# The low parts of some weights made by an accumulating DMA instead of VectorE

## The chip, the cores and the metric

The kernel runs on one core of a Trainium2 chip. The metric is the device time of one execution in microseconds, as the median over runs. Engines are named as in the profile: PE (TensorE), ACT (ScalarE), DVE (VectorE), POOL (GpSimd), SP (SyncE, which here only issues DMAs).

## The reference

A decoder trunk of two layers on 512 tokens of width 1024. In each layer the normalised input is multiplied by one wide projection whose columns feed four mixers of 512 channels, each with a gate:

```
h = rms_norm(x, norm_g[layer])
a_u, a_g, qd, kd, vd, b_g, c_x, c_g, m_q, m_g = split(h @ w_in[layer], 10)
y_a = s5_mixer(a_u, ...)            # complex state-space scan, GELU, GLU
y_b = diff_attention(q, k, v, lam)  # two softmaxes, their difference
y_c = rglru_mixer(c_x, ...)         # convolution, gated linear recurrence
y_m = memory_attention(m_q, ...)    # 256 memory tokens
mixed = concat(y_a * silu(a_g), y_b * silu(b_g), y_c * silu(c_g), y_m * silu(m_g))
x = x + mixed @ w_out[layer]
```

A last normalisation gives the output. Everything is float32.

## The kernel before

The large products are made in three passes on PE to keep float32 accuracy: each operand is split into a high part (rounded to the format fp32r) and a low part (what the rounding left), and a product is high x high + high x low + low x high. The activations are split once per layer (hThi, hTlo). The weights are split as they stream in.

The weights come in 136 pieces of 128 partitions x 1024 floats (512 KB), 68 for each layer, in a hand-written order of groups: in layer 0 q v k kv cx au cg bg mq ag mg gl and the output projection, in layer 1 q k cx v kv au mq bg mg ag cg gl and the output projection. cg, bg, mq, ag and mg are the gates and the memory query; each has 4 pieces, so the five have 20 pieces in a layer. They come after au, the input of the state-space mixer, so they are multiplied while that mixer (function s5, with many small VectorE operations on tiles u, xr, xp, wt, kq) runs, and in layer 0 also the end of the attention and the linear recurrence (function lru). A piece of these five groups gives 24 matmuls of 512 columns at L508 (cm_block).

One piece takes this way. SP loads it into a tile raw (two buffers; w_load, L152). ACT rounds it into whi (three buffers; L166). DVE subtracts whi from raw and gives wlo (three buffers; L172). Then raw is free, and SP loads the piece after the next one. When PE comes to piece i, w_use asks for the splits up to piece i+2, so both copies run two pieces ahead of PE; a whi or wlo buffer is free again once PE has left the piece three before.

Side work is written as generators (class Streams) that are stepped between groups of matmuls; each engine then works its instructions in a fixed order made when the program is built. POOL does little: it clears a few tiles, loads block-diagonal weights (bd, L1080), and at L966 issues for each of the four blocks of s5 8 small copies from kq to MT, which wait for DVE's kq.

Of the kernel before, what the change touches and what calls it, by code (L numbers as in the profile page):

```python
# [13 lines left out]
AF = mybir.ActivationFunctionType  # L14
ALU = mybir.AluOpType
# [14 lines left out]

ORDER = ["q v k kv cx au cg bg mq ag mg gl oAM0 oAM1 oBC0 oBC1".split(),
         "q k cx v kv au mq bg mg ag cg gl oAM0 oAM1 oBC0 oBC1".split()]

C_ID, C_DM, C_IF, C_KEEP, C_CM, C_END = 0, 128, 144, 152, 152, 280

# [55 lines left out]
def tile_kernel(ctx: ExitStack, tc: tile.TileContext, A, out):  # L91
    nc = tc.nc
    V, S, G, PE = nc.vector, nc.scalar, nc.gpsimd, nc.tensor
# [11 lines left out]
    def nm(s):  # L105
        uid[0] += 1
        return f"{s}_{uid[0]}"
# [26 lines left out]


    pieces = []
    wbuf = {}
    loaded = [0]
    split = {"hi": 0, "lo": 0}
# [2 lines left out]
    def w_dma(upto):  # L142

        while loaded[0] < min(upto, len(pieces)):
            w_load(loaded[0])
            loaded[0] += 1

    def w_load(i):
        src = pieces[i]
        raw = wpool.tile([P, 1024], F32, tag="raw", bufs=NRAW, name=nm("raw"))  # L150
        if len(src.shape) == 3:
            nc.sync.dma_start(out=raw.rearrange("p (a b) -> p a b", a=src.shape[1]), in_=src)  # L152
        else:
            dst = raw.rearrange("p (a b c) -> p a b c", a=src.shape[1], b=src.shape[2])
            for j in range(src.shape[2]):
                nc.sync.dma_start(out=dst[:, :, j], in_=src[:, :, j])
        wbuf[i] = raw

    def w_split(i, pool_):

        while split[pool_] < min(i + 1, len(pieces)):
            j = split[pool_]
            split[pool_] += 1
            if pool_ == "hi":
                hi = wpool.tile([P, 1024], F32R, tag="whi", bufs=NHI, name=nm("whi"))
                S.copy(hi, wbuf[j])  # L166
                wbuf[j] = (wbuf[j], hi)
            else:
                w_split(j, "hi")
                raw, hi = wbuf[j]  # L170
                lo = wpool.tile([P, 1024], F32R, tag="wlo", bufs=NLO, name=nm("wlo"))
                V.tensor_tensor(out=lo, in0=raw, in1=hi, op=ALU.subtract)  # L172
                wbuf[j] = (hi, lo)
                w_dma(j + NRAW + 1)

    def w_use(i):
        w_split(i + NHI - 1, "hi")
        w_split(i + NLO - 1, "lo")
        return wbuf.pop(i)
# [23 lines left out]
    COL = {n: i * GW for i, n in enumerate(["au", "ag", "q", "k", "v", "bg", "cx", "cg", "mq", "mg"])}  # L203

    def add(l, n, u, ps_):
        plan.append((l, n, u, list(range(len(pieces), len(pieces) + len(ps_)))))
        pieces.extend(ps_)

# [8 lines left out]
    for l in range(DEPTH):  # L217
        for n in ORDER[l]:
            if n == "kv":
                for u in range(2):  # L220
                    add(l, "mk", u, cm_pieces(A["w_mem_kv"][l], 256 * u))
                add(l, "mv", 0, tm_pieces(A["w_mem_kv"][l], 512))
            elif n == "gl":
                w = A["s5_w_glu"][l].rearrange("(k p) (s c) -> p k s c", p=P, s=2)
                for u in range(2):
                    add(l, "gl", u, [w[:, 2 * i:2 * i + 2, :, 256 * u:256 * u + 256] for i in range(2)])
            elif n[0] == "o":
                ps_ = []
                for g in n[1:3]:
                    r0 = 512 * "ABCM".index(g)  # L230
                    ps_ += tm_pieces(w_out[l, r0:r0 + 512], 512 * int(n[3]))
                add(l, "o", n[1:], ps_)
            elif n in ("q", "k", "v", "au"):
                add(l, n, 0, tm_pieces(w_in[l], COL[n]))
            else:
                for u in range(2):
                    add(l, n, u, cm_pieces(w_in[l], COL[n] + 256 * u))
# [24 lines left out]
    for l in range(DEPTH):  # L262
        nc.sync.dma_start(out=vec[65:81, l].rearrange("q (g c) -> q g c", g=2)[:, :, 0:16],
                          in_=A["s5_d"][l].rearrange("(q g) h -> q g h", g=2))
# [53 lines left out]
    for t in range(NT):  # L318
        h, hn = hn, (norm_h(t + 1) if t + 1 < NT else None)
        transpose_split(h, cur["hi"], cur["lo"], t * 128)  # L320
        if t < 2:
            w_split(t, "lo")
# [49 lines left out]
    for bits in (5, 8, 10, 24):  # L372
        e = math.floor(math.log2(rest))
        q = 2.0 ** (e - bits)
        c = math.floor(rest / q) * q if bits != 24 else float(np.float32(rest))
# [726 lines left out]
    for pi, (l, n, u, ids) in enumerate(plan):  # L1102
# [93 lines left out]
        elif n == "gl":  # L1196
# [4 lines left out]
            for hf, pid in enumerate(ids):  # L1201
                whi, wlo = (w.rearrange("p (k s c) -> p k s c", k=2, s=2) for w in w_use(pid))
                for j in range(2):
                    for s in (1, 0):
                        a = gacc[j][s]
# [9 lines left out]
                    if hf == 1:  # L1215
                        V.scalar_tensor_tensor(out=th, in0=th, scalar=1.0, in1=a, op0=ALU.add, op1=ALU.mult)
                        ag = R["ag"][:, 2 * u + j, :]
# [4 lines left out]
        if n == "o":  # L1222
# [29 lines left out]
            hi = lambda k, t, gs=gs: gs[k // 4][0][:, k % 4, t * 128:(t + 1) * 128]  # L1252
            lo = lambda k, t, gs=gs: gs[k // 4][1][:, k % 4, t * 128:(t + 1) * 128]
# [69 lines left out]
```

## Time and profile before

| | us |
|---|---|
| median of 3 runs | 934.51 (934.37 to 934.92) |
| the profiled execution, its own time | 934.99 |
| its span, first to last instruction | 933.2 |
| PE busy | 908.3 (97%) |
| DVE busy | 645.2 (69%) |
| ACT busy | 521.4 (56%) |
| POOL busy | 42.8 (5%) |

A matmul's record overlaps with the next one's, so PE is called busy when it works without a gap; the idle time of PE in a stretch is the stretch less PE's busy time. The shares are means over stages with very different loads, which is why the rows below go by stretches. PEclk is the share of TensorE's full clock that was granted.

### The profile page before, as it was taken

Reading aid. Unit: us, or ns where it says so; the run is one execution under the profiler, and the core shown is the slowest. Engines: PE = TensorE matmul, PEld = TensorE weight load, DVE = VectorE, ACT = ScalarE, POOL = GpSimd, SP = SyncE. Lnnn points to the kernel's source line nnn. Section 1 sums busy time; section 2 is a strip of 40 time slices with the busy share of each in tenths; the row PEclk is TensorE's granted clock in tenths of the full one; section 3 lists DMA queues with packets and bytes.
Section 4 is the critical chain, followed back from the end, with each engine's and each line's share of the span. In section 5 each row is a group of like instructions: output and inputs, shape, how many; then the busy total and the mean of one; then the engine's idle time right before and its main releaser. Section 6 shows DMA issues by size and latency. Waiting matters only on the chain.

```text
span 933.2 us, 12492 instructions
## 1 busy us (share of the span) xinstructions
PE 908.3 (97%) x4538; PEld 751.0 (80%) x4538; DVE 645.2 (69%) x1297; ACT 521.4 (56%) x1038; POOL 42.8 (5%) x94
## 2 busy tenths in 40 slices
PE   6999999999999989999999999999999999999997
PEld 4788878877888878888888888788778888788885
DVE  6975877458999965893373675853698998667343
ACT  6674776987343355831454579665646333764123
POOL 1001000001011100000100000000101110000000
PEclk9999999999999999999999999999999999999999
DMA  5833432103213225532343321421212222243222
GB/s 198 210 103 99 137 91 68 46 23 94 68 50 116 71 69 186 142 113 91 106 162 105 91 91 46 147 89 59 72 48 70 72 72 68 68 155 117 93 88 91
DMA packets 81072, 90.59 MB, mean 97 GB/s; under 512 B 23793, under 2 KB 58226, under 8 KB 81010
## 3 DMA queue, kind: packets, MB, share of 16 engines
q1 hardware_dynamic: 77986, 85.98, 29.8%
q10 hardware_dynamic: 720, 2.62, 0.8%
q0 software_dynamic: 2304, 1.18, 0.5%
q8 instruction: 36, 0.59, 0.3%
q14 instruction: 26, 0.21, 0.1%
HBM read 84.92 MB, written 4.19 MB: 95 GB/s over the span
## 4 chain that ended last, share of the span: by engine, by line
PE 78%; DVE 14%; ACT 4%; DMA 2%; issue 2%; SPq 1%; DVEq 0%; ACTq 0%
PE acc L528 37%; PE acc L508 19%; PE acc L1209 5%; DVE u L340 3%; PE sc L639 2%; DVE wlo L172 2%; PE ms L672 2%; PE tp L1032 1%; PE sc L638 1%; DVE xr L1015 1%; PE sc L640 1%; PE tp L826 1%; PE tp L305 1%; PE tp L662 1%; PE sc L801 1%
## 5 line engine op out<-in xcount | busy, mean ns | idle before, releaser
L166 ACT CAST whi<-raw 128x1024 fp32r<-128x1024 f32 x136 | 143.2, 1053 | 224.4 <-PE acc L528 123.8
L172 DVE TENSOR_TENSOR wlo<-raw,whi 128x1024 fp32r<-128x1024 f32 x136 | 166.1, 1222 | 120.8 <-ACT whi L166 120.3
L508 PE MATMUL acc<-hThi,whi 128*128 128x512 f32 x384 | 155.3, 404 | 0.3 <-DVE bg L709 0.3
L508 PE MATMUL acc<-hThi,wlo 128*128 128x512 f32 x384 | 153.1, 399 | 0.0
L508 PE MATMUL acc<-hTlo,whi 128*128 128x512 f32 x384 | 152.7, 398 | 0.0
L528 PE MATMUL acc<-whi,hThi 128*128 128x512 f32 x256 | 105.1, 410 | 0.8 <-ACT whi L166 0.8
L528 PE MATMUL acc<-wlo,hThi 128*128 128x512 f32 x256 | 101.7, 397 | 0.0
L528 PE MATMUL acc<-whi,hTlo 128*128 128x512 f32 x256 | 101.1, 396 | 0.0
L528 PE MATMUL acc<-whi,mxl 128*128 128x512 f32 x256 | 100.2, 391 | 0.0
L528 PE MATMUL acc<-whi,mxh 128*128 128x512 f32 x256 | 100.2, 391 | 0.0
L528 PE MATMUL acc<-wlo,mxh 128*128 128x512 f32 x256 | 100.2, 391 | 0.0
L508 PEld LDWEIGHTS acc<-hThi,wlo 128*128 128x128 f32 x384 | 72.6, 189 | 14.2
L508 PEld LDWEIGHTS acc<-hThi,whi 128*128 128x128 f32 x384 | 72.7, 189 | 13.5 <-DVE bg L709 0.7
L508 PEld LDWEIGHTS acc<-hTlo,whi 128*128 128x128 f32 x384 | 72.8, 190 | 12.9
L528 PEld LDWEIGHTS acc<-whi,hThi 128*128 128x128 f32 x256 | 56.4, 220 | 8.9 <-ACT whi L166 1.2
L528 PEld LDWEIGHTS acc<-whi,hTlo 128*128 128x128 f32 x256 | 56.3, 220 | 7.7 <-DVE hTlo L308 0.2
L528 PEld LDWEIGHTS acc<-wlo,hThi 128*128 128x128 f32 x256 | 56.6, 221 | 7.1
L528 PEld LDWEIGHTS acc<-whi,mxl 128*128 128x128 f32 x256 | 48.1, 188 | 9.8
L528 PEld LDWEIGHTS acc<-whi,mxh 128*128 128x128 f32 x256 | 48.1, 188 | 9.7
L528 PEld LDWEIGHTS acc<-wlo,mxh 128*128 128x128 f32 x256 | 48.1, 188 | 9.6
L642 DVE TENSOR_REDUCE mx<-sc 128x2 f32<-128x256 f32 (+3 forms) x32 | 26.3, 823 | 36.3 <-PE sc L640 36.2
L966 POOL DMA_DIRECT2D MT<-kq x64 | 32.1, 508 | 376.3 <-DVE kq L340 233.5
(305 smaller groups left out, 1671.5 us busy)
## 6 DMA issues: line engine op xcount, KB each, us to landing
raw<-in_w_in_dram SPq DMA_DIRECT2D x80, 512.0 KB, 3.6
raw<-in_w_out_dram SPq DMA_DIRECT2D x32, 512.0 KB, 3.3
raw<-in_w_mem_kv_dram SPq DMA_DIRECT2D x16, 512.0 KB, 3.3
x<-in_x_dram SPq DMA_DIRECT2D x8, 512.0 KB, 5.2
raw<-in_s_w_glu_dram SPq DMA_DIRECT2D x16, 256.0 KB, 3.1
mt<-in_mem_dram SPq DMA_DIRECT2D x4, 512.0 KB
xd<-x SPq DMA_DIRECT2D x4, 512.0 KB, 4.3
x<-xd SPq DMA_DIRECT2D x4, 512.0 KB, 7.0
```

The costliest lines, as they stand in the source:

```text
L166: S.copy(hi, wbuf[j])
L172: V.tensor_tensor(out=lo, in0=raw, in1=hi, op=ALU.subtract)
L305: lastins["pe"] = PE.transpose(pt[:, k, :], h[:, kk * 128:(kk + 1) * 128], ident)
L340: V.tensor_tensor(out=o, in0=a, in1=b, op=op)
L508: PE.matmul(a[j][:, :ncol], w[:, kk, c], h(k), start=(hf == 0 and i == 0), stop=(hf == 1 and i == 3 * nh - 1))
L528: PE.matmul(a[t], h(k, t), w[:, kk, :], start=(p == 0 and kk == 0 and i == 0), stop=(p == np_ - 1 and kk == 1 and i == 2))
L638: PE.matmul(s[:, m, :M], qh[:, m, h, :], kT[m][:, h, :M], start=True, stop=False)
L639: PE.matmul(s[:, m, :M], ql[own, h, :], kT[m][own, h, :M], start=False, stop=False)
L642: V.tensor_reduce(out=mx, in_=s[:, :, :N], op=ALU.max, axis=AX.X)
L672: PE.matmul(a, pT[:, j, :], v[:, j, h * 128:(h + 1) * 128], start=(j == 0), stop=(j == i))
L966: G.dma_start(out=MT[g * 64 + 64 - n:g * 64 + 64, g, t], in_=kq[g * 64:g * 64 + n])
L1209: PE.matmul(a, w[:, k, s, j * 128:(j + 1) * 128], h[:, 2 * hf + k, :], start=(hf == 0 and i == 0), stop=(hf == 1 and i == 5))
```

## The change

For the pieces of cg, bg, mq, ag and mg (40 of 136) the subtraction on DVE goes away. In its place ACT writes the negated raw piece, rounded to fp32r, into wlo, and a DMA issued by POOL reads the same piece from DRAM a second time and adds it to wlo in place. raw is then read by the two ACT copies alone; wlo is complete when the DMA has landed. A helper (w_view) gives the tile the shape of the piece for both DMAs. All other pieces keep the subtraction.

```diff
+BY_DMA = ("cg", "bg", "mq", "ag", "mg")
...
+    by_dma = set()
...
+    def w_view(t, src):
+
+        if len(src.shape) == 3:
+            return t.rearrange("p (a b) -> p a b", a=src.shape[1])
+        return t.rearrange("p (a b c) -> p a b c", a=src.shape[1], b=src.shape[2])
...
                 lo = wpool.tile([P, 1024], F32R, tag="wlo", bufs=NLO, name=nm("wlo"))
-                V.tensor_tensor(out=lo, in0=raw, in1=hi, op=ALU.subtract)
+                if j in by_dma:
+
+                    S.activation(lo, raw, AF.Copy, scale=-1.0)
+                    G.dma_start(out=w_view(lo, pieces[j]), in_=pieces[j], accum_op=ALU.add)
+                else:
+                    V.tensor_tensor(out=lo, in0=raw, in1=hi, op=ALU.subtract)
...
     def add(l, n, u, ps_):
+        if n in BY_DMA:
+            by_dma.update(range(len(pieces), len(pieces) + len(ps_)))
```

## Rows read from the trace of the kernel before

**Rows 1.** The page: busy time of each engine, and the chain's shares by engine.
```profile
PE 908.3 (97%) x4538; PEld 751.0 (80%) x4538; DVE 645.2 (69%) x1297; ACT 521.4 (56%) x1038; POOL 42.8 (5%) x94
...
PE 78%; DVE 14%; ACT 4%; DMA 2%; issue 2%; SPq 1%; DVEq 0%; ACTq 0%
```
**Rows 2.** Windows, matmuls of L508 alone: stretch, width, PE busy (matmuls), loads, PEclk, DMA.
```profile
191.00:348.00 157.00, 121.61 (x480) 88.66 (x480) 0.99 0.24 73
642.00:809.00 167.00, 119.97 (x480) 87.55 (x480) 1.00 0.21 66
```
**Rows 3.** Windows by stage: width, PE PEld DVE ACT POOL busy (instructions), PEclk, DMA share, GB/s.
```profile
195.00:215.00 20.00, 20.00 (x109) 15.76 (x108) 10.22 (x19) 17.61 (x38) 0.00 (x0) 1.00 0.09 27
215.00:230.00 15.00, 13.79 (x73) 11.21 (x72) 14.94 (x24) 12.58 (x26) 1.69 (x4) 0.91 0.28 85
...
260.00:300.00 40.00, 39.68 (x209) 33.06 (x208) 39.37 (x70) 15.88 (x35) 4.93 (x10) 1.00 0.28 82
300.00:340.00 40.00, 36.99 (x205) 30.66 (x204) 35.59 (x74) 18.07 (x31) 4.01 (x8) 1.00 0.27 82
...
740.00:770.00 30.00, 29.33 (x164) 24.82 (x164) 28.17 (x53) 10.68 (x24) 4.00 (x8) 1.00 0.24 74
770.00:815.00 45.00, 43.60 (x227) 35.55 (x226) 32.08 (x53) 27.10 (x52) 0.00 (x0) 1.00 0.23 71
```
**Rows 4.** The same view of a narrow stretch behind PE's first standstill.
```profile
226.00:231.00 5.00, 5.00 (x23) 4.22 (x22) 4.92 (x10) 4.32 (x9) 2.69 (x6) 0.66 0.37 110
```
**Rows 5.** PE's waits in 180 to 360 us: us in total, times, longest.
```profile
PE tp L1044 <- ACT yf L1046: 1.7, 1, 1.7
PE tp L1032 <- DVE xp L340: 1.3, 2, 0.9
PE tp L948 <- DVE wt L340: 1.2, 1, 1.2
```
**Rows 6.** The chain in order of time, 195 to 232: start, us, what.
```profile
212.54 1.92 ACT li L747
...
215.79 1.14 DVE wlo L172
...
225.80 0.63 PE tp L948 x4
```
**Rows 7.** Groups of VectorE's instructions in 215 to 345 us, the costliest.
```profile
L172 DVE TENSOR_TENSOR wlo<-raw,whi 128x1024 fp32r<-128x1024 f32 x19 | 23.2, 1220 | 1.0 <-ACT whi L166 1.0
```
**Rows 8.** Timeline of ScalarE, 186 to 262: start, us, instruction, [idle before].
```profile
214.37 1.04 ACT L166 CAST whi<-raw 128x1024 fp32r<-128x1024 f32 x1
...
236.91 1.05 ACT L166 CAST whi<-raw 128x1024 fp32r<-128x1024 f32 x1 [6.48 <-PE acc L508]
```
**Rows 9.** GpSimd's DMA issues: the group at L1080, and L966 min/median/max in ns.
```profile
L1080 POOL DMA_DIRECT2D bd<-in_lru_w_a_dram x4 | 2.6, 662 | 0.0
...
L966 POOL DMA_DIRECT2D MT<-kq x64: 488/507/525, 228.3 to 767.3; - x64
```
**Rows 10.** The weight loads of SP (L152), from issue to landing.
```profile
DMA to landing us min/median/max: 3.2/3.5/8.4
```
**Rows 11.** DMA queues in 230 to 320: packets, MB, share of 16 engines; issues.
```profile
q1 hardware_dynamic: 6118, 6.07, 22.0%
...
raw<-in_w_in_dram SPq DMA_DIRECT2D x12, 512.0 KB, 3.5
```
**Rows 12.** The chain in 195 to 345, two of its longest pieces.
```profile
316.98 3.60 DMA raw<-in_w_in_dram
339.69 5.47 PE acc L508 x24
```
**Rows 13.** Timeline of PE: the first matmul of two pieces.
```profile
217.04 0.39 PE L508 MATMUL acc<-hThi,whi 128*128 128x512 f32 x1
...
318.45 0.39 PE L508 MATMUL acc<-hThi,whi 128*128 128x512 f32 x1
```
**Rows 14.** Timeline of GpSimd, 180 to 360: two of its four blocks.
```profile
256.90 4.03 POOL L966 DMA_DIRECT2D MT<-kq  x8 [24.56 <-DVE kq L340]
...
315.12 2.03 POOL L966 DMA_DIRECT2D MT<-kq  x4 [0.19 <-issue]
```

More of the change, by code (lines that the diff above doesn't have):

```diff
@@ L150, in w_load @@
         raw = wpool.tile([P, 1024], F32, tag="raw", bufs=NRAW, name=nm("raw"))
+        dst = w_view(raw, src)
         if len(src.shape) == 3:
-            nc.sync.dma_start(out=raw.rearrange("p (a b) -> p a b", a=src.shape[1]), in_=src)
+            nc.sync.dma_start(out=dst, in_=src)
         else:
-            dst = raw.rearrange("p (a b c) -> p a b c", a=src.shape[1], b=src.shape[2])
             for j in range(src.shape[2]):
```

## The prediction

> **What bounds the kernel now.** The page's head comes first. TensorE is busy for 908.3 of 933.2 us, and the chain that ended last is 78% PE, 14% DVE and 4% ACT [rows 1]. So work taken off VectorE can pay only where PE stands still. The windows by stage say where that is: the width of a window less PE's busy time is PE's idle time. In the stretches in which the weights of this change are used (by PE's matmuls of these pieces, 480 in a layer, layer 0 from 191 to 348 us and layer 1 from 642 to 809 [rows 2]) it is 1.21 us in 215 to 230, 0.32 in 260 to 300, 3.01 in 300 to 340, 0.67 in 740 to 770 and 1.40 in 770 to 815, together 6.6 us [rows 3]. VectorE is busy for 14.94 of 15, 39.37 of 40 and 35.59 of 40 us in the first three [rows 3]. One loss is not idle time: in 226 to 231, just behind the first standstill, the granted clock is 0.66, so PE works for part of it at the lower of its two levels; 5 us at 0.34 less is 1.7 us [rows 4]. All that the change can win is therefore 6.6 + 1.7 = 8.3 us.
>
> The list of PE's waits tells who ends these idle times: VectorE's wt (1.2 us) and xp (1.3 us), and ScalarE's yf (1.7 us), which closes the state-space stage that VectorE has been working off [rows 5]. The chain in order of time shows the first of them: ScalarE's square root until 214.5, then VectorE alone, with weight subtractions of 1.14 us in it, until PE goes on at 225.80 [rows 6]. The subtractions lie on this path as ballast, with no engine waiting for their result.
>
> **What is taken away.** 40 of the 136 subtractions on VectorE, 20 in each layer. In 215 to 345 us there are 19, 1220 ns each by the group [rows 7], and each holds VectorE for 1.14 us by the chain: 19 x 1.14 = 21.7 us out of 130 us in which VectorE hardly rests. That is far more than the 3.3 us of idle PE behind 231, and these waits should go.
>
> **What ScalarE gets.** 40 negated copies of 128x1024, each straight behind its high copy. No such activation is in the trace; a high copy of the same shape takes 1.04 to 1.05 us [rows 8], and I take 1.05. Later than 230 ScalarE has room (in 260 to 300 it works 15.88 of 40 us, in 300 to 340 18.07), so there it costs nothing. In 195 to 215 it works 17.61 of 20 us [rows 3] and is on the chain [rows 6]: two copies in front of the square root are 2.1 us. In exchange two or three subtractions of 1.14 us go from the same path, so PE's wait at 225.80 comes out about the same or 1 us shorter.
>
> **What GpSimd and the DMA get.** 40 issues and 40 transfers that add 512 KB into SBUF. The trace has no accumulating transfer. Issue: GpSimd's small copies take 507 ns (16 to 64 rows) and its block loads 662 ns (64 partitions in 4 runs, so 256 rows) [rows 9]; a weight piece has 512 rows, and along that slope (0.7 ns a row) I take 0.85 us, with 0.66 as the lower bound. Flight: a plain load of such a piece lands 3.5 us after the start of its issue on SP, and 8.4 at worst [rows 10]; the 12 loads in 230 to 320 hold 22.0% of 16 engines for 90 us, thus 317 / 12 / 16 = 1.65 us of each engine for one load [rows 11]. An accumulation reads what it adds to as well, so I count the packets' time twice: 3.5 + 1.65 + 0.45 for the longer issue = 5.6 us from issue to landing. Bounds: 3.9 (a plain load issued by GpSimd) and 10.5 (the slowest load of the trace with both additions). Room on the engines is there, though not much of it: the DMA share is 0.22 to 0.28 in these windows [rows 3], and 20 transfers of 3.3 us in the 157 us of layer 0 add 0.42. That raw loads and accumulations will now meet is part of the upper bound.
>
> Is GpSimd's issue slowed by a busy VectorE? The row says no: its 64 small copies took 488 to 525 ns [rows 9], most of them in windows in which VectorE works nearly all the time [rows 3]. A rule of the Trainium skill speaks against the change at this point: SBUF — State Buffer, section "SBUF: two separate sides", says that a DMA issued by GpSimd starves for descriptors while VectorE runs an operation in a two-port mode. By the trace the sum stays as it is; by the rule the rival on held issues below.
>
> **Is the low part there in time?** From the start of the high copy it is 1.05 + 1.05 + 5.6 = 7.7 us (bounds 6.0 and 12.6) instead of some 2.3 now. A high copy starts when PE has left the piece three before, so PE has two pieces to work on meanwhile: ScalarE stands ready and waits for PE [rows 8]. 24 matmuls of a piece take 5.47 us [rows 12], so that is 10.9 us without any other work between. 7.7 fits into it, and the cover is 3.2 us. It fails where ScalarE is late with the high copy, and that is one place: the fourth piece of cg in layer 0. Its high copy starts at 214.37 [rows 8], PE begins with the piece at 217.04 [rows 13], and now the subtraction has just ended. With two negated copies ahead the high copy starts at 216.5, and the low part lands at 224.2. PE had 217.04 to 231.0 for 14.0 us, of which 1.2 idle and 1.7 clock: 11.0 us of work. I estimate that 3.2 us of it (attention products, transposes, the two products that need no low part) can go first; 7.8 us remain, to 232.0, and with the clock down as before 233.7: **+2.7 us**. Bounds: -2.9 (no wait at all and no fall of the clock) and +7.6 (a flight of 10.5).
>
> **GpSimd's queue.** An accumulation can stand behind a block of 8 small copies, 4.03 us [rows 14]. 7.7 + 4.0 = 11.7 is 0.8 us more than the bare 10.9; other work between the matmuls covers most of these 8 places: **+0.5 us** (0 to 6.4).
>
> **Waits that go.** Layer 0 behind 231: 0.32 + 3.01 = 3.3, of which I take **-2.8**, since the last (yf) also holds the two ScalarE steps themselves. Layer 1: 0.67 + 1.40 = 2.1, **-1.5**; ScalarE is not late there. Loading the raw pieces gets easier, if anything: a buffer is free after the negated copy, with no wait for VectorE's queue; the chain has one such load in it [rows 12], counted in the 3.01.
>
> Sum: +2.7 + 0.5 - 2.8 - 1.5 = -1.1 us. The profiled execution took 934.99 us (span 933.2, 1.8 around it), 0.48 more than the median of 934.51. So **933.4 us**. Below 0.2% (1.9 us) this kernel's measurement can't tell a change from none.
>
> **Rivals.** *The relief pays in full*: the order of instructions on each engine, which is made anew when the program is built, brings the late high copy forward or fills the gap, and the waits go: -8.3 to -3, thus 926 to 931. For it: VectorE is full in every stretch in which PE waits; against: ScalarE's load before 215.
>
> *The accumulations come too late* (slower). Place: GpSimd's queue, in order. The copies of block 3 end only at 317.15 [rows 14], since they wait for VectorE's kq; an accumulation placed behind them lands at 317.15 + 5.6 = 322.8, and PE takes the first piece of mg at 318.45 [rows 13]: +4.3 there. Four such blocks in a layer, about half of them hit, are +8 to +9 and eat the gain: 937 to 943. It decides from the point at which issue, flight and queue together pass 8.8 us (10.9 less the two copies). For it: such waits of GpSimd are long today; against: VectorE, and with it kq, gets 21.7 us earlier.
>
> *Accumulation is slower than any row here*: flights over 14 us would hold every piece at half of 16 us or more, above the mean 7.8 us that a piece takes now (157 us for 20 [rows 2]): 945 to 1000. Nothing in the trace speaks for it or excludes it.
>
> *Issues are held by VectorE* (slower). If each issue of GpSimd had to wait for the end of one VectorE operation, 1.22 us for the longest common one [rows 7], the low part would take 8.9 us and still fit into 10.9, but the late piece would cost 1.2 us more, and a block of 8 copies 9.8 us more, which makes some of the accumulations behind blocks late: about 2 us more in all 8 places. -1.1 + 1.2 + 2 = +2.1: 936.6. The even 507 ns speak against it [rows 9]. [...]
>
> *Nothing moves*: VectorE's relief is taken up by other waits of the same stage, 933 to 936.
>
> **How the numbers follow.** Forecast with its parts, 930 to 937: 0.42 (of it faster 0.17, same 0.16, slower 0.09). Full relief 0.20. Late accumulations 0.20. Beyond all rows 0.08. Held issues 0.04. Nothing moves 0.06. So faster 0.37, same 0.22, slower 0.41. The forecast's own range is 930 to 937; the range 926 to 944 takes in full relief and late accumulations too and leaves out what lies beyond the rows and a rest at the edges, under 2 in 10.
>
> **What would show it.** In the profile after: 96 subtractions on VectorE; 40 negated copies of about 1.05 us; 40 accumulations on GpSimd, issue 0.7 to 1 us and landing 4 to 7 us; PE's waits for wt, xp and yf gone; one new wait of PE for a low part near 217 us. I am wrong if landing takes over 9 us, if PE's waits for wlo are spread over many pieces, or if GpSimd's issue is several us long.

## The result, and the profile after

The changed kernel takes 940.47 us (median; 939.31 to 941.62) beside 934.5 for the kernel before: a ratio of 1.0063, 95% interval 1.0047 to 1.0079. It is slower by 6 us. The forecast was 933.4 us with a range of 926 to 944: the time went up where a small gain was forecast, and it lies inside the range. The profiled execution took 939.66 us, of which 937.9 are its span.

The page of the kernel after: busy time by engine, the DMA queues, and the chain's shares by engine.

```profile
PE 908.1 (97%) x4538; PEld 751.2 (80%) x4538; DVE 604.0 (64%) x1257; ACT 557.1 (59%) x1076; POOL 95.8 (10%) x134
...
q1 hardware_dynamic: 77986, 85.98, 29.8%
q0 software_dynamic: 23424, 22.16, 15.6%
...
PE 76%; DVE 8%; issue 6%; DMA 4%; ACT 2%; POOL 2%; SPq 1%; DVEq 0%; POOLq 0%
```

The change did what it says: VectorE works 41 us less than in [rows 1] (40 subtractions), ScalarE 36 us more, and the chain's share on VectorE falls from 14% to 8%. PE's busy time is the same as in [rows 1], yet the span is 4.7 us longer, so the loss is idle time of PE. Here is where it idles: the windows by stage, columns as in [rows 3]; the last two are narrow ones, the first standstill and what follows it.

```profile
195.00:215.00 20.00, 18.47 (x90) 14.51 (x89) 8.78 (x16) 18.01 (x35) 2.57 (x2) 0.91 0.54 106
230.00:260.00 30.00, 27.18 (x148) 22.67 (x147) 27.36 (x58) 19.97 (x38) 10.71 (x18) 1.00 0.72 143
260.00:300.00 40.00, 37.99 (x202) 31.87 (x202) 37.45 (x75) 16.82 (x27) 12.40 (x15) 1.00 0.70 137
300.00:340.00 40.00, 38.59 (x212) 32.93 (x211) 22.68 (x49) 22.11 (x32) 10.61 (x13) 1.00 0.73 150
...
195.00:197.10 2.10, 0.59 (x3) 0.22 (x2) 2.10 (x3) 2.10 (x4) 0.20 (x1) 0.90 0.00 0
197.10:200.00 2.90, 2.87 (x8) 2.40 (x9) 0.84 (x3) 2.90 (x7) 1.09 (x1) 0.50 0.74 200
```

Of the kernel before, [rows 3] has these windows but one:

```profile
230.00:260.00 30.00, 29.99 (x165) 25.81 (x164) 28.92 (x56) 9.81 (x16) 5.42 (x12) 0.99 0.22 68
```

195 to 215 had no idle time and now has 1.53 us and a granted clock of 0.91; 230 to 260 goes from 0.01 to 2.82; 260 to 300 from 0.32 to 2.01; only 300 to 340 gains clearly (3.01 to 1.41). In 197.1 to 200 the granted clock is 0.50, the lower of the two levels (1.2 GHz), right behind the standstill: 1.45 us of work lost. In exchange the fall of the clock in 226 to 231 [rows 4], 1.7 us, is not there (1.00 in the same stretch after), so by the clock the two kernels lose about the same, and the difference is idle time: 8.6 us in 195 to 340, 4.5 before. The list of PE's waits in 180 to 360, which answers to [rows 5], says who ends these idle times:

```profile
PE tp L1049 <- DVE xp L357: 5.7, 4, 2.2
PE acc L525 <- ACT au L930: 1.5, 1, 1.5
PE acc L525 <- DMA wlo<-in_w_in_dram: 0.8, 1, 0.8
```

The waits for wt and yf of [rows 5] are gone, as forecast. But xp, 1.3 us before, is 5.7, although VectorE has far less to do, and there is a new wait for ScalarE's au copies. The new operations themselves (groups of ScalarE and GpSimd; issues with their median landing):

```profile
L184 ACT ACTIVATE wlo<-raw 128x1024 fp32r<-128x1024 f32 x40 | 42.5, 1062 | 3.5 <-PE acc L545 3.5
L185 POOL DMA_DIRECT2D wlo<-in_w_in_dram x40 | 52.1, 1302 | 335.0 <-ACT wlo L184 286.9
...
raw<-in_w_in_dram SPq DMA_DIRECT2D x80, 512.0 KB, 3.6
wlo<-in_w_in_dram POOLq DMA_DIRECT2D x40, 512.0 KB, 7.0
```

Where in the program was the time lost? PE's first transposes of layer 1 (tp<-cst,h) are a milestone that every kernel passes. The timeline of PE, kernel before and then kernel after:

```profile
469.43 0.65 PE L305 MATMUL tp<-cst,h 128*128 128x128 f32 x4
```
```profile
473.76 0.65 PE L322 MATMUL tp<-cst,h 128*128 128x128 f32 x4
```

The milestone is 4.33 us later, and from there to the end it is 463.8 us before (933.2 - 469.43) and 464.1 after. So all but 0.4 us of the loss lies in layer 0, and layer 1, with as many subtractions less, gained nothing.

**First place: ScalarE's order at 195.** The timeline of ScalarE after, and that of PE:

```profile
194.59 1.05 ACT L176 CAST whi<-raw 128x1024 fp32r<-128x1024 f32 x1
195.53 1.07 ACT L184 ACTIVATE wlo<-raw 128x1024 fp32r<-128x1024 f32 x1
196.48 1.08 ACT L930 COPY au<-acc 128x512 f32<-128x512 f32 x2
```
```profile
195.36 0.23 PE L657 MATMUL sc<-cmb,idb 128*128 128x128 bf16 x1
197.13 0.80 PE L525 MATMUL acc<-hThi,whi 128*128 128x512 f32 x1 [1.53 <-ACT au L930]
```

The au copies empty PE's accumulators (tiles acc). They now stand behind a high copy and a negated copy of cg; PE has no free accumulator and waits 1.53 us. In the kernel before, ScalarE came to the same high copy and to the first au copy 8 us earlier:

```profile
186.88 1.05 ACT L166 CAST whi<-raw 128x1024 fp32r<-128x1024 f32 x1
187.81 0.60 ACT L913 COPY au<-acc 128x512 f32<-128x512 f32 x1
```

Of the 8.67 us by which the first au copy is later, the negated copy itself is only about 1 us; the high copy ahead of it already comes 7.71 us later. The order of the instructions on each engine is made anew when the program is built, and in the new order ScalarE first works off activations of the attention and of the recurrence that stood behind the au copy before. This goes with the place of the negated copies of cg of layer 0: in the five kernels that have them on ScalarE (after, e1, e4, e9, e10) the first au copy is at 196.0 to 196.7, in the eight others at 187.6 to 188.7.

**Second place: GpSimd's queue and VectorE's kq.** GpSimd's timeline after, where the kernel before has one block of 8 small copies without a gap, as in the first line of [rows 14], and VectorE's timeline after:

```profile
223.61 1.28 POOL L185 DMA_DIRECT2D wlo<-in_w_in_dram  x1 [5.08 <-ACT wlo L184]
225.99 1.28 POOL L185 DMA_DIRECT2D wlo<-in_w_in_dram  x1 [1.10 <-ACT wlo L184]
228.93 3.08 POOL L983 DMA_DIRECT2D MT<-kq  x6 [1.67 <-DVE kq L357]
232.97 0.53 POOL L983 DMA_DIRECT2D MT<-kq  x1 [0.96 <-DMA wlo<-in_w_in_dram]
236.69 0.52 POOL L983 DMA_DIRECT2D MT<-kq  x1 [3.20 <-DMA MT<-kq]
```
```profile
239.18 0.22 DVE L357 TENSOR_TENSOR kq<-pv,cst 128x64 f32<-128x64 f32 x1 [2.00 <-DMA MT<-kq]
```

Two accumulations stand ahead of the block. The seventh copy starts when the first of them has landed (223.61 + 9.08 = 232.69), the eighth when the second has (225.99 + 10.4 = 236.4; the profile names a small copy as its releaser): 4.2 us together. kq has two buffers, so VectorE, which works in order, can write the next kq only when copies of an earlier one have landed. It stands for 2.00 us in front of an operation of 0.22 us (and 0.9 us once more at 263.5), and a wait of PE for xp, 2.2 us, follows at 248.8. The chain of after takes the same way: the accumulation of 223.61, which lands after 9.08 us, and then the copy at 232.97.

Here too the order has a share. In the kernel before, VectorE comes to this write of kq only 38 us behind the block's first copy (228.31):

```profile
266.71 0.21 DVE L340 TENSOR_TENSOR kq<-pv,cst 128x64 f32<-128x64 f32 x1
```

In the kernel after it is 10 us behind (239.18, the first copy at 228.93), and in e6, which has the relief alone, 7 us (234.74 and 227.36). So with the relief VectorE comes to the write about when the copies land.

### The profile page after: what moved, and what is told of

Read it like the earlier page. It is cut to its first block, busy times and chain, and to the rows that moved or that the text cites. A ratio compares the mean times of both kernels' runs of the same rounds, so it can differ in the third digit from the quotient of the medians.

```text
span 937.9 us, 12582 instructions
## 1 busy us (share of the span) xinstructions
PE 908.1 (97%) x4538; PEld 751.2 (80%) x4538; DVE 604.0 (64%) x1257; ACT 557.1 (59%) x1076; POOL 95.8 (10%) x134
## 4 chain that ended last, share of the span: by engine, by line
PE 76%; DVE 8%; issue 6%; DMA 4%; ACT 2%; POOL 2%; SPq 1%; DVEq 0%; POOLq 0%
PE acc L545 37%; PE acc L525 19%; PE acc L1226 5%; PE sc L656 2%; DVE u L357 2%; DMA wlo<-in_w_in_dram 2%; PE ms L689 2%; PE sc L655 1%; PE tp L843 1%; PE tp L1049 1%; PE sc L818 1%; PE sc L657 1%; PE tp L322 1%; POOL wlo L185 1%; POOL MT L983 1%
## 5 line engine op out<-in xcount | busy, mean ns | idle before, releaser
L187 DVE TENSOR_TENSOR wlo<-raw,whi 128x1024 fp32r<-128x1024 f32 x96 | 117.2, 1221 | 120.4 <-ACT whi L176 119.8
L185 POOL DMA_DIRECT2D wlo<-in_w_in_dram x40 | 52.1, 1302 | 335.0 <-ACT wlo L184 286.9
```

The lines of the kernel that those rows point to most:

```text
L185: G.dma_start(out=w_view(lo, pieces[j]), in_=pieces[j], accum_op=ALU.add)
```

## Experiments

Each time below is a median of 4 to 11 runs; the kernel before, run beside them, took 934.60, 934.51 and 934.96 us in the three sets. The milestone is the start of PE's first transposes of layer 1 in the profiled execution. It comes from one execution: e8 has the median of the kernel before, yet its milestone is 1 us earlier, with the same wait for wt but without the fall of the clock behind it (1.00 in 226 to 231). Differences of milestones can be off by that much.

| kernel | median us | ratio to before (95%) | milestone us |
|---|---|---|---|
| before | 934.5 | | 469.43 |
| after | 940.47 | 1.0063 (1.0047 to 1.0079) | 473.76 |
| e1 eight buffers of kq | 936.21 | 1.0016 (1.0007 to 1.0025) | 470.77 |
| e2 cg of layer 0 keeps the subtraction | 934.21 | 0.9995 (0.9986 to 1.0004) | 468.57 |
| e3 both | 932.75 | 0.9980 (0.9971 to 0.9989) | 467.01 |
| e4 negated copies, no accumulation | 937.29 | 1.0025 (1.0015 to 1.0035) | 471.76 |
| e6 no low parts made | 932.15 | 0.9973 (0.9963 to 0.9984) | 466.56 |
| e7 subtraction on GpSimd | 993.99 | 1.0638 (1.0623 to 1.0652) | 505.32 |
| e8 kernel before, eight buffers of kq | 934.65 | 1.0002 (0.9994 to 1.0011) | 468.45 |
| e9 small copies in SyncE's queue | 945.61 | 1.0104 (1.0085 to 1.0122) | 480.12 |
| e10 e4 with eight buffers of kq | 935.78 | 1.0009 (1.0000 to 1.0018) | 470.16 |
| e11 four negated copies on VectorE | 934.75 | 0.9998 (0.9989 to 1.0006) | 469.21 |
| e12 e11 with eight buffers of kq | 932.08 | 0.9971 (0.9959 to 0.9982) | 466.93 |

The theory has the two places above: the queue (accumulations hold kq) and ScalarE's order. The rivals are the low parts that come late, as in the prediction, and shared DMA engines.

**e1: eight buffers of kq.**

```diff
-            kq = tiny.tile([P, 4, 16], F32, tag="kq", name=nm("kq"))
+            kq = tiny.tile([P, 4, 16], F32, tag="kq", bufs=8, name=nm("kq"))
```

> The changed kernel with eight buffers instead of two for kq, the source of the small copies on GpSimd's queue, so that VectorE never waits for such a copy to land. Queue theory (the accumulations hold up the small copies, these hold kq, and VectorE stands in order behind it until PE waits for xp): VectorE's waits of 2.0 and 0.9 us for the landing of MT are gone, PE's waits for xp in 230 to 300 us fall from some 4 us to under 1.5, time 936.5 to 938.5. ScalarE theory (the negated copies push other work on a full ScalarE; PE stands still at 195 us): no change, 940 to 941. Low parts that come late: no change either.

936.21, 4.3 us less than after, by the depth of one small tile. VectorE's waits for kq on a DMA are gone, though the small copies still land late (median 3.4 us, as in after). PE's waits for xp in 230 to 300 are 2.1 us (4.3 in after), not under 1.5 as the queue theory expected. PE's waits of e1 in 180 to 360:

```profile
PE tp L1049 <- DVE xp L357: 3.3, 4, 1.2
PE acc L525 <- ACT au L930: 1.5, 1, 1.5
PE acc L525 <- DMA wlo<-in_w_in_dram: 1.2, 1, 1.2
```

So the wait of VectorE for kq is a cause. The wait for au stays, as it should if it has another one, and the wait for a late low part stays too.

**e2: cg of layer 0 keeps the subtraction; e3: that and eight buffers of kq.**

```diff
-        if n in BY_DMA:
+        if n in BY_DMA and (l, n) != (0, "cg"):
```

> The changed kernel, but the four pieces of cg in layer 0 keep the subtraction on VectorE. ScalarE theory: PE's standstill at 195 us and the slow clock behind it go, 3 to 3.6 us less than the changed kernel, 936.5 to 937.5. Queue theory: little, since the accumulations of bg still stand before the small copies; 939 to 940.5. Low parts that come late: PE's one wait for a low part near 223 us (1 us with the clock) goes, 939.5.

> Both edits. If both theories hold and their costs add, 933 to 935, that is no slower than the kernel before; if one of them alone holds, the same time as the better one of the two single edits.

934.21 and 932.75. Four pieces of 40 left as they were give back 6.3 us, which is 2 us under the lowest of the expected times. The two gains don't add up: 4.3 us (e1) and 6.3 us (e2) alone, 7.7 us together. In 195 to 215 of e2 PE works without a gap (20.00 us) at the full clock (1.00), as before the change.

But e2 takes away three things for these pieces: a copy on ScalarE, an accumulation ahead of the first block of small copies, and the late low part. So it doesn't tell them apart; e4 and e11 do.

**e4: the negated copies alone; e10: the same with eight buffers of kq.** Both leave the accumulation out, so the low parts of the 40 pieces are not made.

```diff
                     S.activation(lo, raw, AF.Copy, scale=-1.0)
-                    G.dma_start(out=w_view(lo, pieces[j]), in_=pieces[j], accum_op=ALU.add)
```

> The changed kernel without the accumulating DMAs: the negated copies on ScalarE stay, nothing is added to them (the low parts of these 40 pieces are wrong, the work that is left out is the addition). ScalarE theory alone: the loss at 195 us stays, 937 to 939. Queue theory alone: the loss goes and VectorE's relief is left, 931 to 933. Both: about 934 to 936. Low parts that come late: 931 to 933 as well.

> The negated copies alone (the accumulation is left out, so the low parts are wrong) and eight buffers of kq. With two buffers the negated copies alone took 937.3, with eight and the accumulations 936.2. Queue theory as it stands (the accumulations cost through the wait for kq alone): with neither wait nor accumulation the time is that of the eight buffers with accumulations, 935.8 to 936.6. Rival (the accumulations also cost by late low parts and shared DMA engines): 934.5 to 935.5, 1 us or more under it. Rival (the buffers of kq do nothing without accumulations): 937.3.

937.29 and 935.78. Windows of e4: the stall at 195 is there without any accumulation.

```profile
195.00:215.00 20.00, 18.48 (x88) 14.53 (x88) 8.32 (x15) 17.77 (x34) 0.00 (x0) 0.91 0.17 54
```

So it comes from the negated copies on ScalarE; the time of e4 lies where the ScalarE theory alone put it, and that of e10 between the queue theory's range and the rival's. With two buffers of kq the accumulations cost 3.2 us (940.47 - 937.29), with eight of them 0.4 (936.21 - 935.78; 0.8 if each is set against the kernel before of its own set): most of what they cost goes through kq. One thing of e4 fits no expectation: eight buffers of kq save 1.5 us even without accumulations, though they save none in the kernel before (e8). VectorE waits there once for 0.8 us, until 261.69, in front of a write of kq. The profile names no releaser, but the last small copy of the block ahead, at 257.90, lands 3.5 us later, at 261.4. So the early place of the write costs something even when the copies land at their usual pace; the rest of the 1.5 us was not followed.

**e6: the relief alone.** The low part isn't made for the 40 pieces.

```diff
-                    S.activation(lo, raw, AF.Copy, scale=-1.0)
-                    G.dma_start(out=w_view(lo, pieces[j]), in_=pieces[j], accum_op=ALU.add)
+                    lo = hi
```

> Leaves out the low parts of the 40 pieces altogether (the high part is multiplied in their place), so the output is not the reference's and the time is that of the relief alone: no subtraction on VectorE, no negated copy on ScalarE, no accumulation. Theory of two costs (the relief is real, and ScalarE's copies and GpSimd's queue eat it): 930.0 to 932.5, that is 2 to 4.5 us under the kernel before; the negated copies then cost 937.3 minus this time, the accumulations the 3.2 us from 937.3 to 940.5. Rival (VectorE is not what the waits of layers 0 and 1 hang on, so there was little to win): 934 to 935, with PE's waits for xp still 4 us or more.

932.15: 40 subtractions less, and nothing put in their place, give 2.4 us. The milestone is 2.87 us earlier than before, and layer 1 takes 463.7 us, as in the other kernels of the table (463.6 to 464.1) but e7 (486.8) and e8 (465.0). The windows, then the waits of PE in 180 to 360:

```profile
215.00:230.00 15.00, 14.30 (x91) 12.31 (x90) 13.68 (x25) 11.74 (x25) 2.64 (x6) 1.00 0.35 107
230.00:260.00 30.00, 29.09 (x154) 24.34 (x152) 29.20 (x60) 15.02 (x32) 5.40 (x11) 1.00 0.25 75
260.00:300.00 40.00, 39.21 (x218) 33.13 (x217) 34.35 (x69) 14.15 (x28) 4.00 (x8) 1.00 0.22 69
300.00:340.00 40.00, 39.02 (x206) 32.88 (x205) 25.35 (x52) 18.16 (x25) 4.02 (x8) 1.00 0.23 76
```
```profile
PE tp L1048 <- DVE xp L356: 2.7, 4, 1.0
```

Beside [rows 3] the idle time in 215 to 340 falls only from 4.55 to 3.38 us: 300 to 340 gains 2.03 us, but 230 to 300 loses 1.37. The other 1.7 us of the 2.87 are the clock, which stays at 1.00 in 226 to 231. Without the subtractions PE still waits for VectorE's xp, four times in layer 0. One reading, which no run separates: PE works off the same matmuls sooner and comes earlier to a chain of small operations that depend on each other.

**e7: the subtraction on GpSimd.**

```diff
-                    S.activation(lo, raw, AF.Copy, scale=-1.0)
-                    G.dma_start(out=w_view(lo, pieces[j]), in_=pieces[j], accum_op=ALU.add)
+                    G.tensor_tensor(out=lo, in0=raw, in1=hi, op=ALU.subtract)
```

> The subtraction itself goes to GpSimd (raw minus high part), with no negated copy and no DMA. ScalarE theory: no wait for the au copies at 195 and clock 1.00 in 195 to 215, as with the subtraction on VectorE. Queue theory: the small copies from kq are issued behind subtractions of some 2 to 4 us (an estimate from GpSimd's 0.66 us rows, with twice the elements or more) instead of behind landings of 7 us, so the wait of VectorE for kq is under 1 us. Both together: 932 to 936. Rival (the subtraction on GpSimd is so long, or takes so much from VectorE, that low parts come late): 938 to 950, with PE waits for wlo from POOL.

993.99, far above every expectation, the rival's 938 to 950 too. The low parts aren't what is late (one PE wait of 0.3 us for them); VectorE is. GpSimd's group, then VectorE's and GpSimd's timelines:

```profile
L184 POOL TENSOR_TENSOR wlo<-raw,whi 128x1024 fp32r<-128x1024 f32 x40 | 98.8, 2471 | 339.8 <-ACT whi L176 322.1 <-ACT yg L1050 14.0 <-PE ms L688 3.7
```
```profile
224.11 3.38 DVE L767 TENSOR_TENSOR_SCAN li<-lr,xc 128x512 f32<-128x512 f32 x1
...
227.99 1.21 DVE L767 TENSOR_TENSOR_SCAN li<-lr,xc 128x512 f32<-128x512 f32 x1
```
```profile
224.05 2.36 POOL L184 TENSOR_TENSOR wlo<-raw,whi 128x1024 fp32r<-128x1024 f32 x1 [1.01 <-ACT whi L176]
```

The same scan takes 1.21 us alone and 3.38 when a subtraction on GpSimd is running as it starts. VectorE's busy time is 661.7 us here and 603.4 in e6, and PE waits 22.7 us for xp in layer 0. Part of the loss is the clock, which is 0.91 in 195 to 345: PE's busy time is 924.5 us, 16 us more than before. The Trainium skill, SBUF — State Buffer, section "SBUF: two separate sides", says that a VectorE operation with two SBUF inputs and a GpSimd operation that reads SBUF exclude each other for a whole instruction; these rows agree with it.

**e8: the kernel before with eight buffers of kq** (the line of e1).

> A control: the kernel before with eight buffers of kq instead of two. Queue theory: the kernel before has no wait for kq to lose, so 934.6, within 0.4. Rival (two buffers of kq are a limit by themselves, and the gain of the eight has nothing to do with the accumulations): 931 to 933.5.

934.65: no gain. Two buffers are enough in the order of the kernel before, where the write of kq stands 38 us behind the first copies. By itself this doesn't show that it is the accumulations that make two buffers too few: the relief moves the write, and e4 and e10 gain from eight buffers without accumulations.

**e9: the small copies in SyncE's queue.**

```diff
-                    G.dma_start(out=MT[g * 64 + 64 - n:g * 64 + 64, g, t], in_=kq[g * 64:g * 64 + n])
+                    nc.sync.dma_start(out=MT[g * 64 + 64 - n:g * 64 + 64, g, t], in_=kq[g * 64:g * 64 + n])
```

> The changed kernel with the small copies from kq issued by SyncE's queue instead of GpSimd's; kq keeps its two buffers. Queue theory (the copies are late because they stand behind accumulations that have to land): VectorE's waits for kq go, the copies land within 1.5 to 3 us, and the time is that of the eight buffers, 935.5 to 937. Rival (traffic: the accumulations make every small copy land late, whichever queue it is in): the waits for kq stay 2 us or more and the time 939 to 942. A third way: the copies stand behind a raw load that waits for its buffer, and kq is later still, over 942.

945.61: the third way, and the rival too. SyncE's waits of e9 in 225 to 345; then, of the whole run, VectorE's wait and the landing of MT:

```profile
SPq L983 <- DVE kq L357: 20.5, 4, 9.5
```
```profile
  DVE kq L357: 7.0, 4
...
DMA to landing us min/median/max: 1.6/4.5/6.5
```

SyncE stands 20.5 us for kq with the raw loads queued behind it. And the copies are no sooner there: they land after 4.5 us although no accumulation is in their queue, against 1.6 in e4 without accumulations. Raw loads share that queue, but the chain of e9 has a copy that starts after the raw loads ahead of it have landed (the next is issued at 237.14) and still takes 4.08 us:

```profile
235.07 4.08 DMA MT<-kq
```

So the order in GpSimd's queue isn't the only reason that kq is held; with accumulations under way the copies land late in another queue as well. What is left is the load on the DMA engines: in 220 to 245 us of the kernel after, GpSimd's queue q0 holds 60.0% and q1 27.9% of the 16 engines, where they held 1.6% and 26.6% before. That the load is the cause is argued from these shares; a run that has the load without the queue's order, and nothing else moved, wasn't made.

**e11: the negated copies of cg of layer 0 on VectorE; e12: that and eight buffers of kq.** All 40 accumulations run.

```diff
-                    S.activation(lo, raw, AF.Copy, scale=-1.0)
+                    if j in cg0:
+                        V.tensor_scalar(out=lo, in0=raw, scalar1=-1.0, scalar2=None, op0=ALU.mult)
+                    else:
+                        S.activation(lo, raw, AF.Copy, scale=-1.0)
```

> The changed kernel with the negated copies of cg of layer 0 (4 of the 40) on VectorE instead of ScalarE; the accumulations stay all 40. ScalarE theory (the copy at 195.5 stands before the au copies on ScalarE): no PE wait for the au copies at 197, clock 1.00 in 195 to 215, and 936.5 to 937.5, some 3.5 us less than the changed kernel's 940.5; the waits of VectorE for kq stay 1 us or more, since the accumulations ahead of the first copies stay. Rival (the subtractions taken off VectorE before 230 matter more than ScalarE's order): 939 or more.

> The same, and eight buffers of kq: all 40 accumulations run, with only the order on ScalarE and the wait for kq mended. If the two causes are the whole of it, 932.3 to 933.5, as with cg of layer 0 left to the subtraction (932.75), and PE starts layer 1 within 1 us of 467. Rival (the four accumulations of cg of layer 0 cost by themselves, through late low parts): 934 to 936, with a PE wait for wlo from DMA.

934.75 and 932.08. Four instructions on another engine, with the order that comes with it, are worth 5.7 us (2 us more than expected), and the mended kernel is as fast as the one that makes no low parts at all. It is faster than the kernel before by 0.29%. A window of e12, its first au copy, and its waits of PE in 180 to 360:

```profile
195.00:215.00 20.00, 20.00 (x109) 15.68 (x108) 11.19 (x21) 18.16 (x38) 1.28 (x1) 1.00 0.41 76
```
```profile
187.83 0.60 ACT L936 COPY au<-acc 128x512 f32<-128x512 f32 x1
```
```profile
PE tp L1055 <- DVE xp L363: 2.2, 3, 1.2
PE tp L1053 <- DMA MT<-kq: 1.3, 1, 1.3
PE tp L971 <- DVE wt L363: 0.7, 1, 0.7
PE acc L531 <- DMA wlo<-in_w_in_dram: 0.2, 1, 0.2
```

The au copy is back where the kernel before has it. No wait for au, the clock full, and the wait for a low part, the prediction's largest loss, down to 0.2 us with all accumulations in place. The late landing of the small copies now shows directly: PE waits 1.3 us for MT.

## Why the prediction was wrong

A ladder of four steps leads from before to after, by medians and by the milestone: relief alone (e6) -2.4 us and -2.87; 36 negated copies on ScalarE, 4 on VectorE, and all accumulations, with room for kq (e12), -0.1 and +0.37; kq back to two buffers (e11) +2.7 and +2.28; the last four copies to ScalarE (after) +5.7 and +4.55. The four milestone steps add up to the 4.33 us. (The medians are from different sets, whose runs of the kernel before differ by up to 0.45 us, and a milestone can be off by about 1 us.)

**The step that failed: "What ScalarE gets".** It saw that ScalarE is full in 195 to 215 [rows 3] and then set the price at the one place that the chain showed, the square root in front of PE's wait at 225.80 [rows 6], and offset it with VectorE's subtractions there. That wait is gone from the list, as is the fall of the clock behind it. So the step put the negated copies at about nothing, by the order of the kernel before. What it didn't ask is what else waits for ScalarE there, and whether the order would stay. It is the au copies, which free PE's accumulators, and PE had no idle time there that could warn [rows 3]; and the order did not stay, which brings them 8.67 us later. The prediction knew that the order is made anew, but weighed it only as a reason for a larger gain, in its first rival. The bill was 1.53 us of waiting and 1.45 us at the lower clock, and by the milestone 4.55 us for four copies (3.84 with eight buffers of kq, e1 beside e12). Of the 4.55 us, 4.1 lie in 195 to 340: the 1.45 us, and 2.66 us more idle time than in e11 (8.61 and 5.95), of which the 1.53 us are a part. What share the new order has in the rest, and what the negated copies would have cost in the old one, no run shows.

**"GpSimd's queue", and the rival on it, had the direction wrong.** Both asked whether an accumulation comes late because it stands behind small copies: +0.5. The opposite happened. Small copies come late because accumulations stand ahead of them and are under way, and kq with two buffers hands that on to VectorE: +2.3 to +3.0 at the milestone (e11 beside e12, after beside e1). The argument "VectorE, and with it kq, gets 21.7 us earlier" looked at the writing of kq only; its buffers come free when the copies land, and an earlier write runs into that. The rival's time of 937 to 943, and with it the whole range, holds the result by another way than the rival's own: that is luck.

**The late fourth piece of cg: mechanism right, size wrong.** +2.7 was the largest term of the sum. The wait is there, for DMA as forecast, and is 0.83 us. PE's first matmul of the piece, and the one that waits for the low part:

```profile
222.67 0.39 PE L525 MATMUL acc<-hThi,whi 128*128 128x512 f32 x1
...
224.13 0.50 PE L525 MATMUL acc<-hThi,wlo 128*128 128x512 f32 x1 [0.83 <-DMA wlo<-in_w_in_dram]
```

The forecast landing, 224.2, is met, by two errors that cancel: the high copy started at 214.95, not 216.5, and from there to the landing it took 9.1 us, not 7.7. What was off is PE: it begins the piece at 222.67, not at 217.04 [rows 13], 3.0 us of this by the standstill and the clock at 195. And the term kept the fall of the clock at 226, which did not come.

**The relief.** Layer 0: forecast -2.8, by e6 -2.87, and the agreement is luck. The term was 2.8 us of the 3.3 us of waits behind 231; in e6 the idle time in 230 to 340 falls by 0.66 us only (3.34 to 2.68), and the wait for xp grows. The rest is 0.51 us of idle time in 215 to 230 and the 1.7 us of the clock, which the prediction had counted as staying. Layer 1: forecast -1.5, measured nothing in any kernel; the idle time that [rows 3] shows in 740 to 815 is still there in e6 (30 - 29.26 and 45 - 43.68 us, by waits for xp, yf and u), although VectorE works 49.2 us in that stretch instead of 60.3. Of the 8.3 us that the prediction set as the most that can be won, the relief alone gives 2.4.

**The new operations.** The negated copy: 1.06 us (1.05). Issue of an accumulation: 1.30 us (0.85, and 0.7 to 1 expected: the slope of the nearest rows was too flat). Landing: 7.0 us median, 5.9 to 10.4 (5.6, bounds 3.9 to 10.5). DMA engines: 15.1% of 937.9 us more in q0, over 40 transfers, is 3.5 us of each engine (3.3). The rival of issues held by VectorE did not come: GpSimd's small copies took 507 ns in the median [rows 9] and take 526 now. The rule that the prediction weighed there (the Trainium skill, SBUF — State Buffer, section "SBUF: two separate sides") is on VectorE operations in a two-port mode, and no run here shows whether VectorE ran in one. Low parts were hardly late: PE's waits for them are 1.0 us in the whole run.

## What to carry to other kernels

When work is moved to an engine with spare time, list what else waits for that engine at each place, not only what the chain shows there: the four copies that hurt held back accumulator copies that had never made PE wait. Where the order of the instructions is made anew with each build, compare the orders before and after first: a sum made on the old order may be about a program that no longer exists. A transfer that is hidden for its own consumer can still hold others in flight beside it; look which small buffers are freed by a landing, and deepen those first. And measure the gain first by leaving the work out altogether: here it was 2.4 us of 934, for 40 of 136 subtractions on an engine that looked full.

## What the runs showed of the hardware

An accumulating transfer of 512 KB lands 7.0 us after its issue starts, twice a plain load (3.6), and takes 3.5 us of each DMA engine where a plain load takes 1.65. In GpSimd's queue of the kernel after, the ninth transfer in a row started only when the first had landed (223.61 + 9.08 = 232.69, start 232.97), and the tenth when the second had (236.4, start 236.69). In e7 a VectorE operation with both inputs in SBUF that met a running GpSimd subtraction of 2.36 us was stretched by about its length (3.38 against 1.21 us); one with an input in PSUM (u<-sc,tsq at 247.97) kept its 0.68 us beside another (the kernel puts the tile sc in PSUM).
